# Page starts in SBUF: half pages moved behind the pages, and 128 bytes of padding

## The chip, the core and the metric

The kernel runs on one core of a Trainium2 chip. A core has a matmul engine (PE, whose weight loads are listed apart as PEld), three engines for element-wise work (DVE, ACT, POOL), a queue engine that starts most transfers (SP), and 16 DMA engines. SBUF is the on-chip memory of 128 partitions; an address below is a number of bytes from the start of a partition. The metric is device microseconds for one execution of the whole program; less is better.

## What is computed

A two-layer diffusion backbone over 1024 latent tokens and 256 context tokens, width 1024, all in float32. Cut to what matters:

```
layer 0: h = rmsnorm(x)*(1+scale)+shift ; q,k,v,z = h @ w_in (1024 x 5120)
         o = softmax over [sink, 256 context keys, latent keys within +-128] (16 heads, 4 KV heads)
         x1 = x + gate * ((o * silu(z)) @ w_out)            (2048 x 1024)
layer 1: a,gl,z = rmsnorm(x1) modulated @ w_in (1024 x 6144)
         u = depthwise_conv31(a * sigmoid(gl)) ; u = silu(layernorm(u))
         out = rmsnorm(x1 + gate * ((u * silu(z)) @ w_out)) (2048 x 1024)
```

## The kernel before

**Products.** Every large product is done as three matmuls. An operand is split into a high part, rounded to the matmul's format, and a low part, the rest; the kernel adds high x high, high x low and low x high (`mm3`). In such a matmul the *moving* operand streams 512 columns past the array, and the *stationary* operand, 128 x 128 values, was loaded into it before by a weight load. Both are read from SBUF; the sum goes to PSUM. So one output of 512 columns over 8 slices of 128 inputs is a pass of 24 matmuls. Two of the three have the same stationary operand.

- The stage of the attention projections and the attention itself (about 100 to 820 us): `gemm_half` multiplies a chunk of `w_in` (tiles `whi`, `wlo`, stationary, slice `kt` at byte 512 x kt of its page) with the normed input (tiles `hh`, `hl`, moving, a 2048-byte half of a page). Its matmuls are dealt out in portions of 12 to 15 (`fill`, FILL = 12) between the score matmuls, the transposes and the value matmuls of the attention steps.
- The attention's output projection (about 820 to 980 us, `proj_attn`): `ozh`, `ozl` stationary, `woh`, `wol` moving; for each pair of inputs `kk` and block of 128 tokens six matmuls, four blocks after each other.
- The conv layer's input projection (about 980 to 1540 us, `b_mm`): 48 chunks of weights times 2 token halves, each a pass of 24 matmuls in an unbroken row, `whi`, `wlo` stationary, `h2h`, `h2l` moving. Beside it DVE and POOL run the depthwise convolution of the chunks before (`conv_dve`, `conv_pool`), 31 taps on vector engines.
- The conv layer's output projection (about 1540 to 1750 us, `proj_out`): `gs` pages stationary (high part in the first half of the page, low part in the second), `woh`, `wol` moving; again six matmuls to a block, four blocks.

**Memory.** Nearly all tiles live in *pages*, 45 of 4096 bytes a partition (class `Pages`, `pg`, L114), handed out by a queue of free numbers: the longest free page goes out next. Scratch of 512 to 528 values lives in 6 *half pages* of 2112 bytes (`hp`, L115). Constants live in the pool `cpool` ahead of them. Both kinds of page are tiles of one pool, `pgpool`, which lays its tiles down in the order of their first use. The first uses alternate: half pages come between pages. Since 2112 is 2048 + 64, every half page shifts the pages behind it by 64 bytes against multiples of 2048. In the built program:

| pages | start modulo 2048 | first tiles in them |
|---|---|---|
| 1 | 0 | the zeros of the dummy matmuls (`spin`) |
| 2 to 10 | 64 | first modulation weights, x, first weight chunk |
| 11 to 16 | 128 | modulation weights, weight chunks |
| 17 to 20 | 192 | modulation weights |
| 21 to 45 | 256 | the rest |

All starts are multiples of 64. The half pages begin at 1920, 1984, 0, 64, 128 and 192 modulo 2048. After the first use the free queue mixes the pages, so any tile may later lie in any of them. Which page each tile gets is fixed when the program is built.

**Order.** What each engine runs, and in which order, is fixed at build time; PE's row in particular is written out by hand (`pin`, `InOrder`). Buffers and waits follow the page numbers.

## Time and profile before

| | us |
|---|---|
| median of three runs | 1755.87 |
| lowest and highest run | 1755.66 and 1757.35 |
| the profiled execution's own time | 1756.24 |
| its span, first to last instruction | 1754.5 |
| what lies around the span | 1.7 |

The mean granted TensorE clock of the profiled execution is 0.995. In the profile's tables a group of instructions is named by what it writes and reads, "out<-in", with the buffer numbers left out; psg, pso and pss are the PSUM tiles. The duration of one matmul in these tables runs from its start to its modelled end, and matmuls overlap, so how fast PE goes is read from the distance between starts: the chain of waits lists unbroken rows of matmuls as one piece with its length and count. All times are in us from the start of the span unless said.

### The profile page before, as it was taken

To read this page: it belongs to the slowest core of one execution; us is meant where nothing else is said; L and a number is where in the kernel's file an instruction comes from. 1 tells how busy PE (TensorE), PEld (TensorE's weight loads), DVE (VectorE), ACT (ScalarE), POOL (GpSimd) and SP (SyncE) were. 2 spreads that over 40 slices of the span, in tenths; PEclk is the share of its full clock that TensorE was granted. 3 is DMA by queue.
4 is the path that set the end of the run, shared out by engine and by line. 5 is a ranking of instruction groups with operands and counts; after the bars stand their busy time and mean duration, and the time that the engine had idled before them with its cause. 6 is when DMAs were issued, how large, how long until landed. Compare 5 with 4: busy or idle time off the path is not lost.

```text
span 1754.5 us, 23940 instructions
## 1 busy us (share of the span) xinstructions
PE 1721.4 (98%) x8420; PEld 1424.8 (81%) x8420; DVE 1108.6 (63%) x2095; ACT 891.5 (51%) x1548; POOL 896.1 (51%) x741
## 2 busy tenths in 40 slices
PE   7999999999999999999999999999999999999997
PEld 4688888888888788888888888888888888788886
DVE  6755553555345453555315179999999999867823
ACT  7555553455355444545334355554665564466831
POOL 0255654566646564653101257998898888130300
PEclk9999999999999999999999999999999999999999
DMA  9334442444334442436776633011121202376971
GB/s 306 107 88 140 134 136 81 145 152 145 94 108 147 144 142 80 142 116 203 267 250 243 242 95 104 18 49 36 42 79 37 90 30 79 120 250 242 329 264 48
DMA packets 195324, 242.45 MB, mean 138 GB/s; under 512 B 11798, under 2 KB 126790, under 8 KB 195204
## 3 DMA queue, kind: packets, MB, share of 16 engines
q1 hardware_dynamic: 188516, 230.10, 39.7%
q10 hardware_dynamic: 6688, 10.83, 2.5%
q8 instruction: 66, 1.08, 0.3%
q14 instruction: 54, 0.44, 0.1%
HBM read 188.70 MB, written 41.69 MB: 131 GB/s over the span
## 4 chain that ended last, share of the span: by engine, by line
PE 87%; DMA 6%; DVE 2%; POOL 2%; ACT 2%; issue 1%; SPq 1%; ACTq 0%; DVEq 0%; POOLq 0%
PE psg L89 45%; PE pss L89 22%; PE pso L89 19%; DMA araw_page<-in_ada_w_dram 1%; DMA low_page<-in_conv_w_out_dram 1%; DMA rope_half<-rope_half 1%; POOL rope_half L89 1%; SPq L89 1%; DMA x_page<-in_x_dram 1%; DMA low_page<-in_attn_w_out_dram 0%; DMA wolC<-low_page 0%; DMA wraw_page<-in_attn_w_in_dram 0%; POOL low_page L89 0%; ACT lhi_half L89 0%; DVE ptlo L89 0%
## 5 line engine op out<-in xcount | busy, mean ns | idle before, releaser
L89 POOL TENSOR_TENSOR odd_half<-odd_half,prod_half 128x513 f32<-128x513 f32 (+2 forms) x252 | 313.2, 1250 | 23.9 <-ACT prod_half L89 10.7
L89 PE MATMUL psg<-hh_page,whi_page 128*128 128x512 f32 x600 | 237.8, 396 | 0.0
L89 PE MATMUL psg<-hl_page,whi_page 128*128 128x512 f32 x600 | 237.4, 396 | 0.0
L89 PE MATMUL psg<-hh_page,wlo_page 128*128 128x512 f32 x600 | 237.2, 395 | 0.0
L89 POOL TENSOR_TENSOR wlo_page<-wraw_page,whi_page 128x512 fp32r<-128x512 f32 (+1 forms) x106 | 178.7, 1702 | 96.9 <-ACT whi_page L89 67.6
L89 ACT ACTIVATE prod_half<-ubuf,dww 128x513 f32<-128x513 f32 (+2 forms) x252 | 165.4, 675 | 110.9 <-POOL odd_half L89 108.6
L89 POOL TENSOR_SCALAR p_page<-p_page,sc 128x640 f32<-128x640 f32 (+1 forms) x128 | 99.3, 776 | 227.5 <-DVE sc L89 224.1
L89 PE MATMUL psg<-h2h_page,whi_page 128*128 128x512 f32 x464 | 183.7, 396 | 0.0
L89 PE MATMUL psg<-h2l_page,whi_page 128*128 128x512 f32 x464 | 182.4, 393 | 0.0
L89 PE MATMUL psg<-h2h_page,wlo_page 128*128 128x512 f32 x464 | 182.3, 393 | 0.0
L89 DVE SCALAR_TENSOR_TENSOR pss<-ubuf,dww,pss 128x512 f32<-128x512 f32 (+3 forms) x270 | 172.7, 672 | 0.1
L89 DVE SCALAR_TENSOR_TENSOR pss<-ubuf,wsum,pss 128x512 f32<-128x512 f32 (+3 forms) x270 | 172.0, 673 | 0.2
L89 DVE TENSOR_TENSOR ptlo<-pss,pthi 128x640 fp32r<-128x640 f32 (+1 forms) x144 | 103.5, 719 | 92.0 <-ACT pthi L89 90.8
L89 ACT ACTIVATE pthi<-pss 128x640 fp32r<-128x640 f32 (+1 forms) x144 | 88.9, 617 | 107.3 <-PE pss L89 101.0
L89 ACT ACTIVATE p_page<-p_page,sc 128x641 f32<-128x641 f32 (+1 forms) x128 | 102.6, 801 | 75.0 <-DVE sc L89 70.4
L89 PEld LDWEIGHTS psg<-hh_page,wlo_page 128*128 128x128 f32 x600 | 113.2, 189 | 26.5
L89 PEld LDWEIGHTS psg<-hh_page,whi_page 128*128 128x128 f32 x600 | 113.2, 189 | 21.0
L89 PEld LDWEIGHTS psg<-hl_page,whi_page 128*128 128x128 f32 x600 | 113.1, 189 | 21.0
L89 ACT ACTIVATE whi_page<-wraw_page 128x1024 fp32r<-128x1024 f32 x88 | 92.7, 1053 | 66.1 <-PE psg L89 25.5
L89 PE MATMUL pso<-h2h_page,whi_page 128*128 128x512 f32 x304 | 119.9, 394 | 0.0
L89 PE MATMUL pso<-h2l_page,whi_page 128*128 128x512 f32 x304 | 119.8, 394 | 0.0
L89 PE MATMUL pso<-h2h_page,wlo_page 128*128 128x512 f32 x304 | 119.8, 394 | 0.0
(244 smaller groups left out, 4061.1 us busy)
## 6 DMA issues: line engine op xcount, KB each, us to landing
wraw_page<-in_conv_w_in_dram SPq DMA_DIRECT2D x48, 512.0 KB
wraw_page<-in_attn_w_in_dram SPq DMA_DIRECT2D x40, 512.0 KB
wol_page<-wolA SPq DMA_DIRECT2D x32, 512.0 KB
wo_page<-in_attn_w_out_dram SPq DMA_DIRECT2D x32, 512.0 KB
wo_page<-in_conv_w_out_dram SPq DMA_DIRECT2D x32, 512.0 KB
wol_page<-wolC SPq DMA_DIRECT2D x32, 512.0 KB
rope_half<-rope_half ACTq DMA_DIRECT2D x80, 128.0 KB
araw_page<-in_ada_w_dram SPq DMA_DIRECT2D x32, 256.0 KB
```

The source lines that it names most:

```text
L89: r = f(*a, **k)
```

## The change

The half pages get a pool of their own, opened behind the pool of the pages, and two constants are made larger so that the constants before the pages end at a multiple of 2048:

```diff
     pgpool = ctx_stack.enter_context(tc.tile_pool(name="pages", bufs=1))
+    hfpool = ctx_stack.enter_context(tc.tile_pool(name="halves", bufs=1))
...
     pg = Pages(pgpool, 45, "page", 1024)
-    hp = Pages(pgpool, 6, "half", 528)
+    hp = Pages(hfpool, 6, "half", 528)
...
-    sink = ctile([P, NH], F32, "sink")
+    sink = ctile([P, 2 * NH], F32, "sink")[:, 0:NH]
...
-    cs = ctile([P, 16], F32, "cs")
+    cs = ctile([P, 32], F32, "cs")[:, 0:16]
```

In the built program all 45 pages begin at a multiple of 2048 (the first at 30720, then every 4096). The six half pages follow at 0, 64, 128, 192, 256 and 320 modulo 2048, so the distance of each to the next, modulo 256, is as it was. The tiles `pthi` and `ptlo` (the attention weights for the value matmuls, later the convolution's input buffers) move from 192 to 0 modulo 256; `ident` stays at 128. The page number that each tile gets, the instructions, their order on every engine and their waits are the same; only addresses differ.

## The prediction

> **What bounds the kernel.** I read the page's busy shares first, then the windows by stage, then the waits of PE. The page's head and its row of DMA slices:

> ```profile
> span 1754.5 us, 23940 instructions
> PE 1721.4 (98%) x8420; PEld 1424.8 (81%) x8420; DVE 1108.6 (63%) x2095; ACT 891.5 (51%) x1548; POOL 896.1 (51%) x741
> DMA  9334442444334442436776633011121202376971
> ```

> The windows; after the length the columns are busy us of PE, PEld, DVE, ACT and POOL, then PE's granted clock, the DMA share and GB/s:

> ```profile
> 100.00:820.00 720.00, 714.45 (x3932) 616.29 (x3932) 364.34 (x816) 346.19 (x739) 404.59 (x366) 1.00 0.41 127
> 820.00:980.00 160.00, 158.35 (x753) 130.30 (x752) 59.11 (x115) 64.34 (x95) 19.94 (x26) 1.00 0.74 258
> 980.00:1540.00 560.00, 558.52 (x2438) 453.51 (x2437) 498.63 (x825) 309.70 (x448) 420.13 (x306) 1.00 0.23 74
> 1540.00:1754.00 214.00, 205.10 (x894) 166.15 (x892) 121.23 (x230) 109.03 (x175) 36.22 (x26) 0.99 0.66 231
> ```

> From 100 us on PE is busy at least 96% of each stage, at a granted clock of 0.99 to 1.00. The longest entries in the list of waits of PE are these two (total, times, longest):

> ```profile
> PE pss L89 <- DVE ptlo L89: 4.1, 2, 3.8
> PE pso L89 <- DVE alo_page L89: 4.1, 6, 2.1
> ```

> So the time is the number of matmuls times the distance from one to the next. The change leaves the number and the order alone. Whatever it does, it does through that distance or through the first 50 us, which hang on DMA.

> **The distance is not the same everywhere.** Six neighbouring pieces of the chain of waits, in the conv output projection (start, length, count):

> ```profile
> 1673.20 2.80 PE pss L89 x12
> 1676.00 1.40 PE pso L89 x6
> 1677.40 1.40 PE psg L89 x6
> 1678.80 2.75 PE pss L89 x12
> 1681.55 1.36 PE pso L89 x6
> 1682.91 1.36 PE psg L89 x6
> ```

> All are the same kind of work: blocks of six matmuls of 512 columns, `woh`/`wol` moving, `gs` stationary. The first three rows are one `kk`, the last three the next. 1.40 us for six is 233 ns each; 1.36 is 227. In the built program the first three read moving pages 43 and 28 (start 256 modulo 2048) and stationary pages 3 and 8 (start 64); the last three read moving pages 21 and 22 and stationary pages 42 and 35, which all start at 256. Where the four pages agree, the row settles on 227 ns after some eight matmuls (the 2.75 for the first twelve); where they don't, it stays higher. The same in the attention's output projection:

> ```profile
> 884.61 5.44 PE pss L89 x24
> 890.05 2.72 PE psg L89 x12
> 892.77 2.77 PE pss L89 x12
> 898.30 2.80 PE pss L89 x12
> ```

> The first two rows read only pages 41, 45, 28 and 37, all at 256: 5.44 / 24 and 2.72 / 12 are both 226.7 ns. The row at 892.77 has page 11 (128) and page 8 (64) among its operands; it takes 231 ns, and the last one, with pages at 64 and 128 too, 233. By page numbers, all nine `kk` of the two output projections that have four such blocks in a row reach 227; the other blocks lie mostly between 229 and 234. Every one of these rows is at a granted clock of about 1.00, so the clock isn't it.

> Those pages agree at 256, not at 0. Two answers of the timeline show the dummy matmuls, which read page 1 alone (start 0) for both operands; the first ends at 18 us, the second at 21:

> ```profile
> 17.08 1.19 PE L89 MATMUL pss<-zerr_page 128*128 128x512 f32 x4
> 17.08 4.13 PE L89 MATMUL pss<-zerr_page 128*128 128x512 f32 x17
> ```

> 13 more matmuls in 2.94 us: 226 ns each. So 0 works like 256, and I take 226.7 ns as the distance that a long row reaches with all pages at one start.

> **Conv input projection.** Here a pass of 24 is one piece. The first and last of 75 pieces, and some between:

> ```profile
> 1082.98 5.56 PE pso L89 x24
> 1121.93 5.51 PE psg L89 x24
> 1127.44 5.58 PE pso L89 x24
> 1255.00 5.58 PE psg L89 x24
> 1493.91 1.68 PE pso L89 x8
> ```

> 74 passes fill 1493.91 - 1082.98 = 410.93 us, 5.553 each. For the first token half, all 21 passes whose weight pages start at 256 take 5.51 or 5.52, as at 1121.93, and those with `whi` at 64 or 128 take 5.55 to 5.59 for the most part (1255.00: `whi` at 64). So the start decides there as well, though half of the activation pages of that half are themselves at 64 to 192. With everything at one start a pass would be 5.44, like the row at 884.61: 0.113 less, and 96 passes give 10.8 us. Whether all of it is kept depends on DVE, the next engine. The window of the unbroken part of the convolution:

> ```profile
> 1030.00:1450.00 420.00, 420.00 (x1834) 341.27 (x1833) 402.32 (x640) 250.51 (x360) 364.37 (x273) 1.00 0.18 55
> ```

> The two largest waits of DVE for PE between 1050 and 1540 us:

> ```profile
> DVE ubuf L89 <- PE pso L89: 3.9, 6, 1.4
> DVE ubuf L89 <- PE psg L89: 2.9, 7, 0.7
> ```

> DVE is busy 402.3 of 420 us. A faster PE can give DVE back only what DVE now waits for PE, 3.9 + 2.9 = 6.8 us; beyond that PE arrives at the layer norm's mean (L1336) before DVE has the sums, and waits. I take **-6.8**, bounds -10.8 (DVE's other waits shrink too) and +2.6 (every pass at the 5.58 of the other half: 0.027 x 96).

> **Output projections.** Each has 768 matmuls of 512 columns. Their distance now, from first and last piece of two unbroken stretches:

> ```profile
> 901.10 2.79 PE psg L89 x12
> 945.47 2.78 PE psg L89 x12
> 1623.32 2.77 PE psg L89 x12
> 1651.06 2.77 PE psg L89 x12
> ```

> 17 pieces of 12 from 901.10 to 948.25 are 231.1 ns each, 11 pieces from 1623.32 to 1653.83 likewise. To 226.7 it is 4.4 x 768 = 3.4 us for each. The transposes and evacuations between break the row a few times, so **-3.1** and **-3.2**; bounds 0 and -3.4.

> **Attention stage.** The projections there, the largest group of PE:

> ```profile
> L89 PE MATMUL psg<-hh_page,whi_page 128*128 128x512 f32 x600 | 237.8, 396 | 0.0
> ```

> Two of their portions in the chain of waits:

> ```profile
> 447.72 2.79 PE psg L89 x12
> 451.76 2.78 PE psg L89 x12
> ```

> With `hl`/`whi` and `hh`/`wlo` there are 3 x 600 matmuls. They come in portions of 12 (the two rows above, 232 ns each) with other matmuls between, so a portion begins unsettled. The price of twelve from a fresh begin with agreeing pages is the 2.75 at 1678.80: 0.035 less than 2.785, times 150 portions is **-5.2**. Bounds: 2.72 a portion (-9.8), and 2.80 (+2.3). The score and value matmuls are shorter or read through `ident` and `pthi`; I give them 0, bounds -1 and +1, since no long row of theirs stands alone.

> **Transfers.** The chain of waits between 6 and 50 us is mostly DMA; its first and last piece:

> ```profile
> 6.41 5.61 DMA araw_page<-in_ada_w_dram
> 41.36 9.05 DMA x_page<-in_x_dram
> ```

> Six such pieces make 38.7 us. If transfers into pages at 128 and 192 are slower, some of it goes. The trace has no pair that differs in nothing else, so I bound it by 0 and a tenth of the pieces, -4, and take **-1**, near the lower end. [...] Later stages have DMA shares of 0.23 to 0.74, and no DMA is among PE's waits, so there it is worth nothing.

> **Other engines.** They read the same pages and show no such spread, as in the answer for the tile `whi` (min/median/max ns), over all its pages:

> ```profile
> L89 ACT ACTIVATE whi_page<-wraw_page x88: 1042/1052/1063, 19.4 to 1518.5; 128x1024 fp32r<-128x1024 f32 x88
> ```

> 2% from end to end, so 0 for them.

> **Sum.** 6.8 + 3.1 + 3.2 + 5.2 + 1 = 19.3 us off the profiled execution's 1756.24 is 1737 us. That execution is 0.4 us above the median, which makes no difference here.

> **Rivals.** (a) *Half the gain.* The stationary slice moves by 512 bytes with every `kt`, and the row might unsettle at each step. For it: passes of the second half stay at 5.58 (1127.44) with weight pages at 256. Against: in the output projections the slice changes by 512 with every block too, and the row stays settled. Price: conv passes at 5.51 (4.1 us), attention half of 5.2, output projections whole: 4.1 + 2.6 + 6.3 = 13 at most, some 10 with DVE: 1746.

> (b) *No change.* The start doesn't act on the distance; what differs between the rows is something that goes with the page. Price 0, and with the 1 us of transfers still 1755 to 1756. Against it are rows that differ in nothing but pages, 1.40 and 1.36. [...]

> (c) *Slower.* All operands settle on the wrong distance: at 1676.00 the row is just as settled, but on 233. If a common start of 0 puts a moving 2048-byte run and the slice of the weights in step at the worse place, every long row goes there: conv 96 x (24 x 0.2333 - 5.553) = 4.5, output projections 2.2 ns x 1536 = 3.4, attention 1.2 x 1800 = 2.2; 1766. It decides from a settled distance above 231.5. The dummy matmuls at start 0 speak against it, but they read one page only.

> (d) *Transfers as well*: the forecast with -4 instead of -1, and DVE's other waits shrinking: 1731.

> **Chances.** Forecast 0.50, (a) 0.28, (b) 0.08, (c) 0.09, (d) 0.05. A change of under 0.2% (3.5 us) can hardly be told from none: faster is forecast, (a) and (d), 0.83; same 0.08; slower 0.09. The range from 1729 to 1757 leaves out (c) and the far part of (d) and of the bounds -10.8 and -9.8.

> **What would show it.** In the chain of waits after: passes at 1082 us and behind at 5.44 to 5.46 instead of 5.51 to 5.58, the rows of the output projections at 2.72 for 12, attention portions at 2.75 or less, a new wait of PE for DVE before the layer norm of some us. Passes that keep a mix of 5.51 and 5.58 speak for (a) or (b), passes all at 5.6 for (c). The forecast is wrong if settled rows don't come about, or if DVE eats more than 4 us of the conv stage.

## The result, and the profile after

The changed kernel takes 1733.50 us, median of four runs (1731.22 to 1736.22), against 1755.76 us for the kernel before (four runs, one more than in the table ahead of the prediction, 1755.53 to 1757.35): a ratio of 0.9872, 95% interval 0.9855 to 0.9889. The profiled execution took 1733.08 us, 23.16 less than the profiled one of before. The forecast was 1737, with a range from 1729 to 1757.

The head of the page after:

```profile
span 1731.3 us, 23940 instructions
PE 1699.9 (98%) x8420; PEld 1427.4 (82%) x8420; DVE 1109.0 (64%) x2095; ACT 889.3 (51%) x1548; POOL 896.0 (52%) x741
```

PE is still the engine that never rests, with 21.5 us less of work in the same 8420 matmuls; the other engines have as much as before. Since PE's row is the same in both traces, the same matmul can be looked up in each, and the difference falls into five terms, from one matmul to the next of the list. The count starts at 0, so the 400th has 400 before it:

| from the matmul | before | after | difference | forecast |
|---|---|---|---|---|
| first to the 400th (the opening) | 94.58 | 93.11 | -1.47 | -1 |
| to the last transpose ahead of the wait for `mask_page` (the attention stage) | 729.29 | 721.02 | -8.27 | -5.2 |
| to the first of the conv input projection | 197.92 | 196.70 | -1.22 | -3.1 |
| to the first of the conv output projection | 541.04 | 530.64 | -10.40 | -6.8 |
| to the last | 179.97 | 178.16 | -1.81 | -3.2 |

Eight matmuls and that wait lie between this transpose and the first matmul of the attention's output projection, which stands at 829.22 before and at 820.03 after; counted to that one, the second and third differences are -7.7 and -1.8.

**The long rows.** The chain of waits after, in the conv output projection (start, length, count), where the forecast had rows of 1.40 and 1.36 beside each other:

```profile
1645.78 2.72 PE pss L89 x12
1648.49 1.36 PE pso L89 x6
1649.86 1.36 PE psg L89 x6
1651.21 2.72 PE pss L89 x12
```

Every block of six now takes 1.36 us, every twelve 2.72: 226.7 ns a matmul, without the 2.75 of a row that has to settle. The attention's output projection:

```profile
884.20 2.72 PE pss L89 x12
886.92 2.72 PE psg L89 x12
```

The conv input projection, with one piece of six passes in it:

```profile
1038.41 32.69 PE psg L89 x144
1071.10 5.44 PE pso L89 x24
1076.54 5.44 PE psg L89 x24
1109.18 5.44 PE psg L89 x24
```

Every pass of the unbroken part takes 5.44 us, for both token halves, where 5.51 to 5.59 stood. In the attention stage, portions between the short matmuls:

```profile
443.55 2.73 PE psg L89 x12
447.54 2.75 PE psg L89 x12
```

Worked out from the starts of all neighbouring matmuls of 512 columns at the full clock, the mean distance went from 232.3 to 228.2 ns in the attention stage, from 230.9 to 227.1 and from 231.0 to 226.8 in the output projections, and from 231.4 to 226.8 in the conv input projection.

**DVE in the conv stage.** The window from its first sum for the layer norm's mean to its last, before:

```profile
1087.20:1500.10 412.90, 412.28 (x1782) 334.41 (x1780) 394.80 (x603) 237.56 (x326) 357.88 (x257) 1.00 0.17 51
```

and after:

```profile
1075.30:1479.90 404.60, 403.80 (x1782) 334.14 (x1780) 394.45 (x604) 237.25 (x326) 357.89 (x257) 1.00 0.17 52
```

The stretch became 8.3 us shorter with the same 394.5 to 394.8 us of DVE in it: DVE's idle time fell from 18.1 to 10.15. Its waits in these windows, before:

```profile
DVE wlo_page L89 <- ACT whi_page L89: 6.6, 5, 2.9
DVE ubuf L89 <- PE pso L89: 3.9, 6, 1.4
DVE ubuf L89 <- PE psg L89: 2.6, 6, 0.7
DVE wlo_page L89 <- issue: 1.8, 3, 1.0
```

and after:

```profile
DVE wlo_page L89 <- ACT whi_page L89: 4.4, 4, 1.7
DVE ubuf L89 <- PE pso L89: 1.2, 2, 0.7
DVE ubuf L89 <- PE psg L89: 0.9, 3, 0.4
DVE wlo_page L89 <- issue: 0.5, 1, 0.5
```

Not only the waits for PE shrank (6.5 to 2.1), but those for ACT and for the issue too (8.4 to 4.9). So PE met no new wait there. Two of PE's waits after 1400 us, as the list after has them:

```profile
PE pso L89 <- DVE vsum_page L89: 1.6, 1, 1.6
PE pso L89 <- DVE r L89: 1.3, 1, 1.3
```

The first was 1.5 before. The second is not in the list before: the transposes of the layer norm's factor for the second token half come before DVE has it ready. It is most of what the last term fell short of the forecast.

**What the third term lost.** Behind the wait for `mask_page` (1.76 us) the clock was lower. The window of 10 us there, after:

```profile
820.00:830.00 10.00, 10.00 (x48) 8.45 (x47) 4.39 (x9) 6.88 (x10) 1.60 (x2) 0.88 1.04 410
```

Five matmuls start 427 ns apart and a sixth 367, instead of 227 (granted clock 0.88 in the window), about 1.1 us, and the short matmuls ahead of them lose some 0.4 more. Before, the wait there was 1.65 us, and the clock behind it 1.00.

**The opening.** The window from 20 to 42 us, before:

```profile
20.00:42.00 22.00, 18.32 (x79) 10.20 (x77) 17.18 (x24) 17.84 (x20) 0.00 (x0) 0.92 1.06 327
```

and after:

```profile
20.00:42.00 22.00, 19.33 (x87) 10.61 (x86) 18.82 (x24) 18.98 (x22) 0.00 (x0) 0.99 1.08 386
```

The DMA engines are full in both (1.06 and 1.08), but move 386 GB/s instead of 327 (last column).

### The profile page after: what moved, and what is told of

It is laid out like the page before. It is cut to its first block, busy times and chain, and to the rows that moved or that the text cites. A ratio compares the mean times of both kernels' runs of the same rounds, so it can differ in the third digit from the quotient of the medians.

```text
span 1731.3 us, 23940 instructions
## 1 busy us (share of the span) xinstructions
PE 1699.9 (98%) x8420; PEld 1427.4 (82%) x8420; DVE 1109.0 (64%) x2095; ACT 889.3 (51%) x1548; POOL 896.0 (52%) x741
## 3 DMA queue, kind: packets, MB, share of 16 engines
q8 instruction: 66, 1.08, 0.3%
## 4 chain that ended last, share of the span: by engine, by line
PE 89%; DMA 4%; DVE 3%; ACT 1%; POOL 1%; issue 1%; SPq 1%; ACTq 0%; DVEq 0%; POOLq 0%
PE psg L89 46%; PE pss L89 23%; PE pso L89 20%; DMA low_page<-in_conv_w_out_dram 1%; DMA rope_half<-rope_half 1%; DMA araw_page<-in_ada_w_dram 1%; DVE alo_page L89 1%; SPq L89 1%; DMA wo_page<-in_conv_w_out_dram 0%; POOL rope_half L89 0%; DVE hf_page L89 0%; POOL low_page L89 0%; ACT hh_page L89 0%; DMA ozf_page<-ozd 0%; ACT lhi_half L89 0%
## 5 line engine op out<-in xcount | busy, mean ns | idle before, releaser
L89 POOL TENSOR_TENSOR odd_half<-odd_half,prod_half 128x513 f32<-128x513 f32 (+2 forms) x252 | 314.2, 1254 | 23.0 <-ACT prod_half L89 9.8
L89 PE MATMUL psg<-hh_page,whi_page 128*128 128x512 f32 x600 | 236.2, 394 | 0.0
L89 PE MATMUL psg<-hl_page,whi_page 128*128 128x512 f32 x600 | 235.1, 392 | 0.0
L89 PE MATMUL psg<-hh_page,wlo_page 128*128 128x512 f32 x600 | 234.4, 391 | 0.0
L89 ACT ACTIVATE prod_half<-ubuf,dww 128x513 f32<-128x513 f32 (+2 forms) x252 | 165.6, 675 | 115.9 <-POOL odd_half L89 111.9
L89 POOL TENSOR_TENSOR wlo_page<-wraw_page,whi_page 128x512 fp32r<-128x512 f32 (+1 forms) x106 | 177.6, 1692 | 89.3 <-ACT whi_page L89 61.5
L89 POOL TENSOR_SCALAR p_page<-p_page,sc 128x640 f32<-128x640 f32 (+1 forms) x128 | 99.3, 776 | 224.3 <-DVE sc L89 212.8
L89 PE MATMUL psg<-h2h_page,whi_page 128*128 128x512 f32 x464 | 182.0, 392 | 0.0
L89 PE MATMUL psg<-h2h_page,wlo_page 128*128 128x512 f32 x464 | 180.8, 390 | 0.0
L89 PE MATMUL psg<-h2l_page,whi_page 128*128 128x512 f32 x464 | 180.7, 389 | 0.0
L89 DVE SCALAR_TENSOR_TENSOR pss<-ubuf,dww,pss 128x512 f32<-128x512 f32 (+3 forms) x270 | 172.7, 672 | 0.1
L89 DVE SCALAR_TENSOR_TENSOR pss<-ubuf,wsum,pss 128x512 f32<-128x512 f32 (+3 forms) x270 | 172.0, 672 | 0.2
L89 DVE TENSOR_TENSOR ptlo<-pss,pthi 128x640 fp32r<-128x640 f32 (+1 forms) x144 | 103.5, 719 | 84.9 <-ACT pthi L89 83.7
L89 ACT ACTIVATE p_page<-p_page,sc 128x641 f32<-128x641 f32 (+1 forms) x128 | 102.6, 802 | 77.8 <-DVE sc L89 73.6
L89 ACT ACTIVATE pthi<-pss 128x640 fp32r<-128x640 f32 (+1 forms) x144 | 88.7, 616 | 102.8 <-PE pss L89 96.4
L89 PEld LDWEIGHTS psg<-hh_page,wlo_page 128*128 128x128 f32 x600 | 113.0, 188 | 24.6
L89 PEld LDWEIGHTS psg<-hh_page,whi_page 128*128 128x128 f32 x600 | 113.1, 188 | 19.4
L89 PEld LDWEIGHTS psg<-hl_page,whi_page 128*128 128x128 f32 x600 | 113.2, 189 | 18.5
L89 ACT ACTIVATE whi_page<-wraw_page 128x1024 fp32r<-128x1024 f32 x88 | 92.5, 1052 | 57.9 <-PE psg L89 20.3
L89 PE MATMUL pso<-h2l_page,whi_page 128*128 128x512 f32 x304 | 118.4, 389 | 0.0
L89 PE MATMUL pso<-h2h_page,whi_page 128*128 128x512 f32 x304 | 118.4, 389 | 0.0
L89 PE MATMUL pso<-h2h_page,wlo_page 128*128 128x512 f32 x304 | 118.3, 389 | 0.0
```

Of the source, the lines that this page charges most:

```text
L89: r = f(*a, **k)
```

## The experiments

"The change" below is the changed kernel as it stands. Each time is a median; a ratio is to the kernel before, run on the same chip.

**The distance by itself.** A kernel that leaves the backbone out and only runs rows of 48 matmuls, here its core; `rh`, `rl`, `wh`, `wl` are the starts of the pages in bytes:

```python
for kt in range(8):
    h = mv[:, kt * 1024 + rh // 4:kt * 1024 + rh // 4 + 512]
    l = mv[:, (8 + kt) * 1024 + rl // 4:(8 + kt) * 1024 + rl // 4 + 512]
    a = st[:, kt * P + wh // 4:kt * P + wh // 4 + P]
    b = st[:, 1024 + kt * P + wl // 4:1024 + kt * P + wl // 4 + P]
    for w, m in ((a, h), (a, l), (b, h)):
        nc.tensor.matmul(o, w, m, ...)
```

> A kernel that leaves the backbone out: after loading one block of x it only runs rows of 48 matmuls in the order of the products (high x high, high x low, low x high, 512 columns, a new 512-byte stationary slice per input slice), one row per pair of starts, moving pages at 0 to 224 bytes and stationary pages at 0 to 224 in steps of 32, then 16 rows with mixed starts, then 16 rows of transposes. Theory 'agreement': a row settles at 226.7 ns per matmul (10.88 us for 48) where moving and stationary pages start alike modulo 256, whatever that start is, so the 8 rows on the diagonal of 64 are at 226 to 228 ns and the others at 229 to 234. Theory 'multiples': only pages that themselves start at a multiple of 256 are fast, so of the 64 rows only the one with both at 0 is at 227 and the row with both at 64 is at 229 to 234. Theory 'moving only' (or 'stationary only'): the eight rows with the moving (stationary) start at 0 are at 227 whatever the other is. Theory 'something else in the page' (no effect of the start): all 64 rows are at one distance.

The rows with the moving pages at 64 and the weights at 0 to 192, from the chain of waits (the names give both starts):

```profile
206.09 10.99 PE m64s0x L58 x48
217.07 11.20 PE m64s32x L58 x48
228.27 10.89 PE m64s64x L58 x48
239.16 11.19 PE m64s96x L58 x48
250.35 11.20 PE m64s128x L58 x48
261.55 11.24 PE m64s160x L58 x48
272.79 11.16 PE m64s192x L58 x48
```

Only the row with both at 64 is at 226.7 ns (10.89 / 48, its first matmuls included). The whole table of 64 depends on the difference alone, weight start minus moving start modulo 256; the means of the last 30 distances of a row:

| difference | 0 | 32 | 64 | 96 | 128 | 160 | 192 | 224 |
|---|---|---|---|---|---|---|---|---|
| ns | 226.7 | 233.3 | 233.3 | 234.5 | 232.3 | 233.3 | 228.9 | 233.3 |

All eight rows of the diagonal are at 226.7, and the other fields of the table lie within 0.5 of this list, except for one (moving at 128, weights at 0: 233.3 where the list has 232.3). Agreement decides, not a multiple of 256. Of the mixed rows, one page of the four being off by 64 is enough:

```profile
740.49 11.13 PE q0q64q0q0x L58 x48
762.82 11.20 PE q64q0q0q0x L58 x48
774.01 11.10 PE q0q0q0q64x L58 x48
```

(order in the names: `rh`, `rl`, `wh`, `wl`), 231 to 233 ns here and 230 to 233 in all twelve rows of mixed starts, though in some of them two of every three matmuls have operands that agree. That is what the kernel before shows as well: its matmuls whose own two pages agree are at 230.6 ns in the conv input projection, hardly under the 231.7 to 232.0 of the others, since their neighbours disagree. Rows at 512 and 1024 agree with 0. Transposes take 109.2 ns at all 16 combinations.

**Half pages alone, a common start of 64, and padding alone.** The edits, the first and second against the change, the third against before:

```diff
-    sink = ctile([P, 2 * NH], F32, "sink")[:, 0:NH]
-    cs = ctile([P, 32], F32, "cs")[:, 0:16]
+    sink = ctile([P, NH], F32, "sink")
+    cs = ctile([P, 16], F32, "cs")
```

```diff
-    cs = ctile([P, 32], F32, "cs")[:, 0:16]
+    cs = ctile([P, 48], F32, "cs")[:, 0:16]
```

```diff
-    sink = ctile([P, NH], F32, "sink")
-    cs = ctile([P, 16], F32, "cs")
+    sink = ctile([P, 2 * NH], F32, "sink")[:, 0:NH]
+    cs = ctile([P, 32], F32, "cs")[:, 0:16]
```

> The half pages in a pool of their own, without the padding: all 45 pages start at 1920 modulo 2048, which is 128 modulo 256. Theory 'agreement': nearly the whole gain, 1733 to 1737 us, conv passes of 24 at 5.44 us. Theory 'multiples': pages at 128 modulo 256 are slow, 1750 to 1766 us, conv passes at 5.55 to 5.60.

> The changed kernel with 64 bytes more of padding: all 45 pages start at 64 modulo 2048, all else as in the change. Theory 'agreement': as the change, 1732 to 1736 us, conv passes at 5.44. Theory 'multiples': 1750 to 1766 us, conv passes at 5.55 to 5.60. The first 100 us tell of the transfers: where PE's row stands at its 400th matmul compared with the change (95.0 us there, 96.5 before): the same if starts at 64 cost the transfers nothing, 1 to 4 us later if they do.

> The padding without the pool of the halves: every page moves by 128 bytes and the pages still disagree among each other as before (25 pages at 384 modulo 2048, 9 at 192, 6 at 256, 4 at 320, 1 at 128). Theory 'agreement': 1754 to 1756 us, no change but about 1 us for the attention weights, which now start at 0 modulo 256. Theory 'multiples': the 25 pages that were at a multiple of 256 lose it, 1758 to 1766 us.

Measured beside 1754.22 of before: the half pages alone 1736.86 (ratio 0.9893, 0.9878 to 0.9908), the common start of 64 1736.40 (0.9890, 0.9874 to 0.9906), the padding alone 1754.93 (1.0003, 0.9994 to 1.0012). A pass of the first and one of the second, both with no page at a multiple of 256:

```profile
1096.78 5.44 PE pso L89 x24
```

```profile
1095.33 5.44 PE pso L89 x24
```

and two of the padding alone:

```profile
1110.22 5.56 PE psg L89 x24
1115.79 5.58 PE pso L89 x24
```

So the pool of the halves carries most of the gain, 1.1% of the 1.3 to 1.4% of the change, and the padding alone none. "Multiples" falls for the matmuls. What the padding adds to the pool of the halves is taken up again with the last group of runs.

The value matmuls show the table inside the kernel: with `pthi` as the moving operand of 512 columns and `kvc` as the weights they went at 227.0 ns in the change (difference 0), 233.3 with the pages at 64 and `pthi` at 0 (difference 64), and 232.3 with the halves alone (192, in short rows that don't settle); before 232.1.

**Forms and short portions.** The same kind of kernel with other columns, bf16, and portions behind four transposes:

> A kernel that leaves the backbone out, again only rows of matmuls. (i) Rows of 48 with 512, 384, 256 and 128 columns, moving pages at 0, weight pages at d = 0, 64, 128, 192: by the rows of the first table the 512-column ones go at 226.7, 233.3, 232.3 and 228.9 ns; if the effect belongs to long streams only, the 256- and 128-column rows are the same for every d, as the score and value matmuls were before and after; if it belongs to every read, each row of 384, 256 and 128 loses about the same 2 to 7 ns. (ii) One stationary slice for the whole row: the same table if only the start modulo 256 counts, another if the step of 512 bytes does. (iii) bf16, 512 columns of 1024 bytes, d from 0 to 224: no expectation from the traces; all alike if the effect belongs to the four-byte format. (iv) Portions of 24, 12 and 6 matmuls behind four transposes, at d = 0 and d = 64: if a row needs some eight matmuls to settle, a portion at d = 0 gains over d = 64 little at 6, about 0.03 us at 12 and about 0.1 us at 24; if the row at d = 0 is settled from its first matmul, the gain is 6.6 ns times the count in each: 0.04, 0.08 and 0.16 us.

```profile
34.27 10.88 PE c512d0x L58 x48
45.15 11.20 PE c512d64x L58 x48
78.50 8.35 PE c384d0x L58 x48
86.85 8.48 PE c384d64x L58 x48
112.09 5.76 PE c256d0x L58 x48
117.85 5.66 PE c256d64x L58 x48
355.66 2.75 PE p12d0x L91 x12
374.87 2.80 PE p12d64x L91 x12
```

With 384 columns agreement gains 3.4 ns over a difference of 64 (173.3 against 176.7; 192 has 173.3 too), with 256 it loses 2.2 (120.0 against 117.8), with 128 it does nothing (111.6). The loss with 256 columns is there in the kernel too: neighbouring context projections went from 117.9 to 119.7 ns, value matmuls from 116.7 to 118.0 and score matmuls from 117.8 to 118.6, 0.7 us in all. One stationary slice for all gives the list of 512 columns again: the step of 512 bytes plays no part. In bf16 all eight differences give 215.8 ns. The portion of 12 at difference 0 settles after six to ten matmuls and costs 2.76 on the mean against 2.80; at 24 it is 5.49 against 5.60, at 6 1.39 against 1.40. So the first of the two expectations for portions holds, that a row needs some eight matmuls to settle.

**Pages 4128 bytes apart.**

```diff
-        t = self.pool.tile([P] + list(shape or [self.words]), dt, ...
+        t = self.pool.tile([P, max(n, self.pitch)], dt, ...)[:, 0:n]
...
-    pg = Pages(pgpool, 45, "page", 1024)
+    pg = Pages(pgpool, 45, "page", 1024, 1032)
```

> The changed kernel with pages 4128 bytes apart: page n starts at 32 n modulo 2048, so that the 45 pages have eight starts modulo 256 and any two operands mostly disagree. Theory 'agreement': the whole gain is gone; rows that disagree go at 231 to 233 ns as in the first table, 231.9 on the mean over the eight differences, which is 0.5 above the 231.4 of before: 1754 to 1759 us. Theory 'the half pages were the trouble, not the starts' (they no longer lie between the pages here): the gain stays, 1732 to 1737.

1757.40 us beside 1755.22 (ratio 1.0016, 1.0007 to 1.0025). The mean distances of the three projections and the attention stage are 231.8 to 232.1, where the table's mean is 231.9. The half pages lie apart here as in the change, and the whole gain is gone.

**DVE with more to do.** In the change, and then in the kernel before, one addition is done twice:

```diff
         tt(V, v[:, 0], e, o[:, off:off + n], ALU.add)
+        tt(V, v[:, 0], e, o[:, off:off + n], ALU.add)
```

> The changed kernel with one addition of each convolution unit done twice on DVE (the same sum written twice): 18 more instructions of 0.4 to 0.68 us, about 11 us more of DVE in the conv stage. Theory of the forecast (DVE can give back only what it waits for PE, 2.3 us between 1030 and 1450 after the change, so the rest is on the path): 7 to 9 us slower than the change, 1740 to 1743, with a wait of PE for DVE before the layer norm's mean. Theory 'all of DVE's waits give way' (8.4 us in that window): 2 to 4 us slower. Theory 'DVE is not near the path': the same time as the change.

> The kernel before with the additional 11 us of DVE in the conv stage (the same addition written twice, 18 times). With the change the same edit cost 8.8 us of new waits of PE before the layer norm's mean. Theory of the forecast (DVE could give back only the 6.8 us that it waited for PE): about 4 us slower than before, 1758 to 1761, PE's wait for the sums 1.5 + 4. Theory 'all of its waits that hang on PE' (the change took 8.9 us out of this stage and left some 2.3, so about 11): 0 to 1.5 us slower, 1754 to 1757, PE's wait for the sums 1.5 to 3.

On the change: 1744.62 us beside 1755.22 of before and 1729.31 of the change itself. On the kernel before: 1766.72 beside 1756.04 (ratio 1.0059, 1.0043 to 1.0074). PE's wait for the sums in the first, and the windows around it (PE stands until 1486.6):

```profile
PE pso L89 <- DVE vsum_page L89: 10.4, 1, 10.4
```

```profile
1480.00:1486.00 6.00, 0.00 (x0) 0.00 (x0) 5.55 (x13) 0.00 (x0) 0.00 (x0) 0.50 0.00 1
1486.00:1496.00 10.00, 9.38 (x28) 6.86 (x29) 7.77 (x14) 3.63 (x7) 0.00 (x0) 0.69 0.00 1
```

and in the second:

```profile
PE pso L89 <- DVE vsum_page L89: 10.3, 1, 10.3
```

The same 8.8 us of new wait in both, and behind it some eight matmuls at half the clock (0.50 and 0.69 in the windows), 2 to 3 us more. In the profiles the conv stage is 11.5 us longer on the change (530.64 to 542.16) and 11.3 on the kernel before (541.04 to 552.33). The wait on the change is the one that the forecast's theory gave; the time is above it, by the clock and by some 4 us of the medians that the profiles don't account for. On the kernel before it is neither theory. The stretch from DVE's first sum to its last, on the kernel before and then on the change, each with the doubled addition:

```profile
1085.90:1507.20 421.30, 411.80 (x1780) 334.08 (x1778) 406.90 (x620) 237.64 (x325) 355.39 (x257) 0.99 0.16 50
1072.80:1485.80 413.00, 403.38 (x1780) 333.80 (x1778) 408.29 (x620) 238.03 (x326) 357.88 (x257) 0.99 0.17 51
```

It became 8.4 us longer in both (412.9 to 421.3, 404.6 to 413.0), with 12.1 and 13.8 us more of DVE in it. So only 3.7 of 18.1 us of idle time gave way to more work in the kernel before, and 5.4 of 10.15 in the change, while PE's 8.3 us had come out of the idle time whole. That fits if most of DVE's waits hang on PE's pace, those that the list gives to ACT and to the issue among them: a faster PE shortens them, and more work for DVE shortens few of them. That reading is argued from the lists of waits; no run takes these waits away by themselves.

**The change again, and everything at 64 and at 128.** The two repeats have no edit; the other two enlarge one constant, so that the attention weights and all pages move together:

```diff
-    sink = ctile([P, 2 * NH], F32, "sink")[:, 0:NH]
+    sink = ctile([P, 3 * NH], F32, "sink")[:, 0:NH]
```

(`4 * NH` for 128.)

> The changed kernel itself once more, for a second profile and a ratio beside the other runs: 1731 to 1737 us. The place of PE's 400th matmul was 96.5 us before and 95.0 with the change, but 97.1 and 97.5 with the pages at 128 and 64, and 95.3 with mixed starts. Theory 'transfers like multiples of 256': again 95.0 within 0.5. Theory 'the start varies from run to run by itself': anywhere from 94.5 to 98.

> The changed kernel a third time, beside the two runs that follow: 1729 to 1736 us, PE's 400th matmul between 94.5 and 95.7 us as in the three profiles so far with pages at multiples of 256 (95.0, 94.8, 95.6).

> The changed kernel with 64 bytes more ahead of the attention weights: these and all pages start at 64 modulo 256, so that every long row agrees, and what differs from the change is only where transfers land. Theory 'transfers don't care': the time of the change run beside it, within 1 us on the median, PE's 400th matmul at 94.5 to 95.7. Theory 'transfers into pages off a multiple of 256 are slower': 1 to 3 us above it, the 400th matmul at 96.5 to 98 (97.5 with pages at 64 before).

> The same with everything at 128 modulo 256. Theory 'transfers don't care': as the change, the 400th matmul at 94.5 to 95.7. Theory 'off a multiple of 256': 1 to 3 us above the change, the 400th matmul at 96.5 to 98 (97.1 with pages at 128 before).

The repeats: 1729.31 us (0.9857, 0.9842 to 0.9871) and, in the other comparison, 1731.34 (0.9860, 0.9842 to 0.9878). Beside the latter everything at 64 took 1734.87 (0.9879, 0.9862 to 0.9897) and everything at 128 took 1735.35 (0.9883, 0.9865 to 0.9901). PE's 400th matmul stands at 94.8 and 93.7 in the repeats, at 95.5 and 96.9 in the other two: 1.8 and 3.2 behind the repeat beside them, though 93.7 is below what was written for it, and 95.5 by itself would pass for "transfers don't care". The windows from 20 to 42 us say it better. The second repeat:

```profile
20.00:42.00 22.00, 19.36 (x88) 10.52 (x86) 18.82 (x24) 19.22 (x22) 0.00 (x0) 1.00 1.09 386
```

everything at 64:

```profile
20.00:42.00 22.00, 18.46 (x84) 10.48 (x82) 17.77 (x23) 16.97 (x19) 0.00 (x0) 1.00 1.10 347
```

and everything at 128:

```profile
20.00:42.00 22.00, 18.37 (x79) 10.33 (x77) 17.57 (x22) 17.09 (x20) 0.00 (x0) 0.92 1.11 344
```

In the profiles of four kernels with pages at a multiple of 2048 (the change, its two repeats, the one with more for DVE) this window moved 383 to 387 GB/s, in those of the eight others 327 to 352. So transfers do care where the pages start, which the long rows on PE don't as long as the starts agree (5.44 us a pass at multiples of 2048 and at common starts of 64 and 128). In these profiles a packet of 512 bytes took 27.0 to 27.1 ns in the first 50 us with the pages at multiples of 2048, and 30.5 to 31.7 with a common start of 64 or 128; one of 1024 bytes 47.1 to 47.7 against 50.6 to 51.5. For 512 bytes that is 13 to 15% more at 64 and 16 to 17% at 128; why it is more, no run shows.

What that is worth in time is less sure. The medians differ by 3.5 and 4.0 us, the places of the 400th matmul by 1.8 and 3.2. The rest of the 6.5 and 5.5 us between the profiled executions lies behind the opening, in the attention stage and behind the wait for `mask_page`, where the clock was halved in the profiles at 64 and at 128 and not in the second repeat (1.00 from 820 to 830 us). And the place of the 400th matmul scatters by itself: the kernel before had it at 96.5, and at 95.3 with the doubled addition, which comes only later; the change, with and without that addition, had it at 93.7 to 95.6. The intervals of the ratios overlap too, so the size stays open between about 1 and 4.

## Why the prediction was right

**The distance.** The step that carried the forecast, that matmuls settle on 226.7 ns where the pages agree and on 229 to 234 where they don't, is shown by the table of starts and by the passes of 5.44. Rival (a), a row that unsettles at each step of 512 bytes, falls with the passes of 5.44 for both token halves, and with the row of one slice that is no faster than the stepping one. Rival (b) falls with the pitch of 4128 bytes. The bf16 rows alone would have borne it out (215.8 ns at all eight differences), the fp32r rows of 512 columns don't (226.7 to 234.5). Rival (c), a settled distance of 233, exists: it is any difference of 32, 64, 160 or 224. The common start of the change has difference 0, so it could not come about. One reading under this step was short: the row at 884.61 reads pages 30, 24, 35 and 21 as well, which also start at 256, so that it says the same.

**Conv input projection, -6.8 forecast, -10.4 measured.** The step that failed is the cap by DVE: it counted as DVE's room only the waits that the list gives to PE, 6.8 us. The waits given to ACT and to the issue shrank as well, so nearly the whole of the distance's 10.8 came through. The bound of -10.8 named this, and the value taken was the other. The sign that went with the cap, a new wait of PE for DVE of some us, didn't come either (1.6 us against 1.5).

**Attention stage, -5.2 forecast, -8.3 measured.** A portion was priced at 2.785 before and 2.75 after. The mean distances are 232.3 and 228.2, so twelve gained 0.049 and not 0.035, about 7.3 us for the 1782 matmuls: many portions don't begin quite unsettled (2.73). The value matmuls of 512 columns, put at 0 with bounds of 1, gave about another 1. That this adds up to 8.3 is partly chance: in the eight profiles with one common start the stage was 5.2 to 10.3 us below the profile of before, and the kernel before with the doubled addition, alike up to there, was 2.1 below it.

**Output projections, -6.3 forecast, -3.0 measured.** The distances came out as priced (3.8 and 4.2 ns, 768 matmuls each, some 6 us). Most of what is missing are two events that the trace of before doesn't have: some 1.5 us of half clock behind the wait at 818 us, and the wait of 1.3 us for the layer norm's factor. Neither is tied to the change strictly: in its second repeat the window from 820 to 830 us has a clock of 1.00, and that stage gained 2.8; and the padding alone, with PE's rows as slow as before, waits 1.2 us for the factor. But both come with it as a rule. Of the eight profiles with one common start six have the half clock there and all eight the wait, 0.7 to 1.8 us; of the four others none has the half clock, and the padding alone has the wait. So the terms left out a cost of 2 to 3 us that comes with the change as a rule; why it arises is not shown.

**Transfers, -1 forecast, -1.5 measured in the profile.** The effect is shown by the rates of 383 to 387 GB/s against 327 to 352; its size in time, between about 1 and 4 us, is not, and -1 lies at the low end of that.

**The sum.** The errors of the terms were of both signs: 3.3 us too much for the output projections, and 7.1 too little for the other three. The sum came out 4 us above the profiled time, so part of its nearness is luck. Rival (d), with a chance of 0.05, was nearer: 1731 (its own terms add up to 1730) against measured medians of 1733.5, 1729.3 and 1731.3, and its second half, DVE's other waits giving way, is what happened.

## What to carry to other kernels

On this chip, give the operands of long rows of fp32r matmuls of 512 columns one start modulo 256 bytes, moving and stationary alike (fp32r is the four-byte format of these matmuls); which start it is doesn't matter to PE (226.7 ns at each of the eight common starts from 0 to 224, 228.9 to 234.5 where they differ), and a multiple of 2048 served the transfers as well (383 to 387 GB/s against 327 to 352). One stray size in a pool (here 2112 bytes among pages of 4096) was enough to lose 1.3% of the time here; print the addresses. Where an engine beside the bound one is nearly full (here DVE, 394.8 of 412.9 us), its idle time says little by itself: ask of each wait whether it hangs on the pace of the bound engine.
